# A batched product of attention heads, with its body put under a manual schedule

## The chip, the cores and the metric

The kernel runs on one core of a Trainium2 chip. The metric is the device time of one execution in microseconds (us). The core has five engines with an instruction stream each: PE multiplies matrices, ACT and DVE copy and convert, POOL does too but works on SBUF alone here, and SP issues the transfers between device memory and SBUF. Transfers are carried by 16 DMA engines.

## The reference

Both inputs are float32 with the shape 8 x 12 x 512 x 64 (batch, heads, rows, channels), the output is float32, 8 x 12 x 512 x 512.

```python
def reference(x, y):
    return np.einsum('bhtc,bhsc->bhts', x, y).astype(np.float32)
```

So for each of 96 heads a 512 x 64 matrix is multiplied by the transpose of another one. 25.17 MB are read and 100.66 MB are written.

## The kernel before, in words

The 96 heads form 12 groups of eight (`NG = 12`); inside a group there are two halves `a` of four heads. The work has two kinds of step.

`load(g)` issues two transfers of 1 MB (L63), y and x of group g, into one 2 MB buffer of the pool `dpool`. This pool has six buffers (`NB = 6`), and the results use the same ones.

`prepare(g)` converts the group to bf16 with four casts on POOL (L81) into two buffers of `bpool` (three in all), issues `load(g + 6)` if there is such a group, and then turns the data so that the channels lie on the partitions: eight PE transposes at a time into one `pt` tile of PSUM (L91 for y, L105 for x; two such tiles exist), which DVE (L97, L111) or ACT (L99, L113) copies into `yT` and `xT`. The two halves of y go first, then the two of x; the first half of each goes to DVE and the second to ACT. `prepare` is a Python generator: it stops after each of the four halves, so that its pieces can be woven into something else.

`result(o, steps)` makes one of 48 output blocks (two heads, 2 MB). It has four steps of four matmuls each (L130) into a `pm` tile of PSUM (three exist), and each step's tile is copied to the output buffer by ACT (L137, steps 0 and 2) or DVE (L139, steps 1 and 3). Ahead of each step it takes one piece from `steps`. At the end SP issues the store (L140).

The program text at the bottom runs the two phases:

```python
    for g in range(NB + 1):
        for _ in prepare(g):
            pass
    for o in range(G * NG):
        g = NB + 1 + o
        result(o, prepare(g) if g < NG else iter(()))
```

In the text, then, groups 0 to 6 are prepared first; the pieces of groups 7 to 11 are woven into results 0 to 4, and results 5 to 47 stand alone.

The order in which each engine gets its instructions is not that of the text, however. The tile framework collects the instructions with their dependencies and their wishes for buffers, and a scheduler at compile time lays out each engine's stream; an instruction that is ready in its model can be put ahead of one that stands before it in the text. Semaphore waits are then added for what has to be waited for. In the trace of this kernel twelve matmuls of result 0 (L130) ran at 13.15 to 18.12 us, among the transposes of group 1, and the first evictions (L137, L139) ran at 61.5 us, behind the copies of group 9 (the tenth L113 at 60.60 us, the tenth L111 at 60.37 us). SP's stream held all 24 loads, and then the 48 stores.

Of the kernel before, what the change touches and what calls it, by code (L numbers as in the profile page):

```python
# [1 line left out]

# [5 lines left out]


@with_exitstack  # L10
def kernel(
    ctx: ExitStack,
    tc: tile.TileContext,
    x: bass.AP,
    y: bass.AP,
    out: bass.AP,
):

    nc = tc.nc
    B, H, T, C = x.shape
    _, _, S, _ = y.shape
    P = 128
    G = 4  # L30
    Q = P // G
    R = T // Q
    NG = B * H // (2 * G)
    K = R // 2
    NB = 6
    fp32 = mybir.dt.float32
    bf16 = mybir.dt.bfloat16
    COPY = mybir.ActivationFunctionType.Copy
    assert C * 2 == P and S == T and R == 16 and 4 * R * C == K * S

    xv = x.rearrange("b h t c -> (b h t c)").rearrange("(g a p n) -> g p a n", a=2, p=P, n=R * C)
    yv = y.rearrange("b h t c -> (b h t c)").rearrange("(g a p n) -> g p a n", a=2, p=P, n=R * C)
    ov = out.rearrange("b h t s -> (b h t s)").rearrange("(o p n) -> o p n", p=P, n=K * S)

    const = ctx.enter_context(tc.tile_pool(name="const", bufs=1))
    dpool = ctx.enter_context(tc.tile_pool(name="dpool", bufs=NB))
    bpool = ctx.enter_context(tc.tile_pool(name="bpool", bufs=3))
    xpool = ctx.enter_context(tc.tile_pool(name="xpool", bufs=NG))
    ypool = ctx.enter_context(tc.tile_pool(name="ypool", bufs=NG))
    ptpool = ctx.enter_context(tc.tile_pool(name="ptpsum", bufs=2, space=bass.MemoryType.PSUM))  # L50
    pmpool = ctx.enter_context(tc.tile_pool(name="pmpsum", bufs=3, space=bass.MemoryType.PSUM))

    def buffer():
        data = dpool.tile([P, K * S], fp32)
        return data

    loaded = {}

    def load(g):
        data = buffer()  # L60
        n = 2 * R * C
        for i, v in enumerate((yv, xv)):
            nc.sync.dma_start(data[:, i * n:(i + 1) * n].rearrange("p (a n) -> p a n", a=2), v[g])  # L63
        loaded[g] = [data[:, i * n:(i + 1) * n].rearrange("p (a r c) -> p a r c", a=2, r=R) for i in range(2)]

    for g in range(NB):
        load(g)

    ident = const.tile([P, P], bf16)
    make_identity(nc, ident)  # L70

    made = {}

    def prepare(g):

        halves = []
        for s in loaded.pop(g):
            b = bpool.tile([P, R, 2, C], bf16)
            for half in range(2):
                rows = slice(half * K, (half + 1) * K)  # L80
                nc.gpsimd.tensor_copy(b[:, rows], s[:, :, rows].rearrange("p a r c -> p r a c"))  # L81
            halves.append(b)
        yb, xb = halves
        if g + NB < NG:
            load(g + NB)
        yT = ypool.tile([P, G * Q, R], bf16)
        xT = xpool.tile([P, K, P, 2], bf16)
        for half in range(2):
            pt = ptpool.tile([P, K, P], bf16)
            for k in range(K):  # L90
                nc.tensor.transpose(  # L91
                    pt[:, k, :], yb[:, half * K + k].rearrange("p a c -> p (a c)"), ident
                )
            dst = yT[:, :, half * K:(half + 1) * K]
            src = pt.rearrange("p k n -> p n k")
            if half == 0:
                nc.vector.tensor_copy(dst, src)  # L97
            else:
                nc.scalar.activation(dst, src, COPY)  # L99
            yield  # L100
        for half in range(2):
            pt = ptpool.tile([P, K, P], bf16)
            for k in range(K):
                e, i = divmod(k, K // 2)
                nc.tensor.transpose(  # L105
                    pt[:, k, :], xb[:, e * K + half * K // 2 + i].rearrange("p a c -> p (a c)"), ident
                )
            dst = xT[:, half * K // 2:(half + 1) * K // 2]
            src = pt.rearrange("p (e i) n -> p i n e", e=2)
            if half == 0:  # L110
                nc.vector.tensor_copy(dst, src)  # L111
            else:
                nc.scalar.activation(dst, src, COPY)  # L113
            yield
        made[g] = (xT, yT.rearrange("p n k -> p (n k)"))

    def result(o, steps):

        g, rest = divmod(o, G)
        a, pair = divmod(rest, 2)  # L120
        xT, yT = made[g]
        ot = buffer()
        otv = ot.rearrange("p (r s) -> p r s", s=S)
        for k in range(K // 2):
            next(steps, None)
            pm = pmpool.tile([P, 2, S], fp32)
            for two in range(2):
                for h in range(2):
                    col = (2 * pair + h) * Q
                    nc.tensor.matmul(  # L130
                        pm[h * 64:(h + 1) * 64, two, :],
                        xT[a * C:(a + 1) * C, 2 * k + two, col:col + Q].rearrange("c n e -> c (n e)"),
                        yT[a * C:(a + 1) * C, (2 * pair + h) * S:(2 * pair + h + 1) * S],
                        start=True, stop=True,
                    )
            if k % 2 == 0:
                nc.scalar.activation(otv[:, 2 * k:2 * k + 2, :], pm, COPY)  # L137
            else:
                nc.vector.tensor_copy(otv[:, 2 * k:2 * k + 2, :], pm)  # L139
        nc.sync.dma_start(ov[o], ot)  # L140
        for _ in steps:
            pass

    for g in range(NB + 1):
        for _ in prepare(g):
            pass
    for o in range(G * NG):
        g = NB + 1 + o
        result(o, prepare(g) if g < NG else iter(()))


# [1 line left out]
_INS = ['x', 'y']  # L153
_OUTS = [((8, 12, 512, 512), 'float32')]


# [23 lines left out]
```

## Time and profile before

| what | value |
|---|---|
| median of 4 runs | 308.24 us (307.89 to 308.72) |
| profiled execution, its time | 307.88 us |
| profiled execution, its span | 306.1 us |
| PE busy | 198.7 us (65%) |
| DVE busy | 145.8 us (48%) |
| ACT busy | 119.2 us (39%) |
| POOL busy | 49.3 us (16%), all of it before 68 us |
| moved by the DMA engines | 126.03 MB, 412 GB/s on average |
| a load, from issue to landing | 18.5 to 18.8 us (1 MB) |
| a store, from issue to landing | 26.2 us (2 MB) |

The span is the time from the first to the last instruction in the profiled execution. Busy times overlap, since the engines work side by side; the shares are averages over the whole span. The time from issue to landing of a transfer has its place in the queue in it. The profile's second part cuts the span into 40 slices of 7.65 us.

### The profile page before, as it was taken

Reading aid. Unit: us, or ns where it says so; the run is one execution under the profiler, and the core shown is the slowest. Engines: PE = TensorE matmul, PEld = TensorE weight load, DVE = VectorE, ACT = ScalarE, POOL = GpSimd, SP = SyncE. Lnnn points to the kernel's source line nnn. Section 1 sums busy time; section 2 is a strip of 40 time slices with the busy share of each in tenths; the row PEclk is TensorE's granted clock in tenths of the full one; section 3 lists DMA queues with packets and bytes.
Section 4 is the critical chain, followed back from the end, with each engine's and each line's share of the span. In section 5 each row is a group of like instructions: output and inputs, shape, how many; then the busy total and the mean of one; then the engine's idle time right before and its main releaser. Section 6 shows DMA issues by size and latency. Waiting matters only on the chain.

```text
span 306.1 us, 2985 instructions
## 1 busy us (share of the span) xinstructions
PE 198.7 (65%) x1152; PEld 107.2 (35%) x1152; DVE 145.8 (48%) x120; ACT 119.2 (39%) x121; POOL 49.3 (16%) x54
## 2 busy tenths in 40 slices
PE   1886666699899857767586757676676757671000
PEld 1555555655355423323232323332332323230000
DVE  0434544499777544545454444445454544443000
ACT  1233344399465352433334342525343443422000
POOL 3776777770000000000000000000000000000000
PEclk9999677599555555555555555555555555555555
DMA  7999999979999999999999999999999999999994
GB/s 282 412 411 408 410 408 408 408 321 441 411 430 422 424 430 420 435 415 441 415 437 419 432 426 418 435 424 430 424 424 430 428 413 441 415 439 420 435 422 206
DMA packets 13455, 126.03 MB, mean 412 GB/s; under 512 B 1152, under 2 KB 1152, under 8 KB 7296
## 3 DMA queue, kind: packets, MB, share of 16 engines
q1 hardware_dynamic: 13440, 125.83, 98.3%
q8 instruction: 9, 0.15, 0.2%
q14 instruction: 6, 0.05, 0.0%
HBM read 25.17 MB, written 100.66 MB: 411 GB/s over the span
## 4 chain that ended last, share of the span: by engine, by line
DMA 57%; PE 19%; ACT 7%; DVE 5%; SPq 1%; issue 1%; POOL 1%; ACTq 0%; DVEq 0%; POOLq 0%
DMA out_dram<-data 51%; PE pm L130 11%; DMA data<-in_x_dram 6%; PE pt L105 4%; ACT data L137 4%; PE pt L91 4%; DVE data L139 3%; ACT xT L113 2%; ACT yT L99 1%; DVE yT L97 1%; SPq L63 1%; POOL b L81 1%; ACTq L137 0%; SPq L140 0%; DVEq L139 0%
## 5 line engine op out<-in xcount | busy, mean ns | idle before, releaser
L130 PE MATMUL pm<-yT,xT 64*64 64x512 bf16 x768 | 159.2, 600 | 56.7 <-ACT data L137 52.2
L139 DVE COPY data<-pm 128x1024 f32<-128x1024 f32 x96 | 117.2, 1224 | 96.6 <-DMA out_dram<-data 56.2
L137 ACT ACTIVATE data<-pm 128x1024 f32<-128x1024 f32 x96 | 94.1, 1022 | 119.0 <-DMA out_dram<-data 107.7
L130 PEld LDWEIGHTS <-xT 64*64 64x64 bf16 x768 | 73.0, 148 | 137.7 <-issue 128.6
L81 POOL CAST b<-data 128x1024 bf16<-128x1024 f32 x48 | 48.6, 1040 | 18.1 <-DMA data<-in_y_dram 8.1
L91 PE MATMUL pt<-ident,b 128*128 128x128 bf16 x192 | 18.8, 272 | 16.8 <-POOL b L81 7.9
L105 PE MATMUL pt<-ident,b 128*128 128x128 bf16 x192 | 21.7, 286 | 6.1 <-DVE yT L97 4.9
L111 DVE COPY xT<-pt 128x1024 bf16<-128x1024 bf16 x12 | 14.7, 1223 | 19.6 <-PE pt L105 19.6
L91 PEld LDWEIGHTS <-b 128*128 128x128 bf16 x192 | 16.7, 125 | 20.1 <-issue 11.9
L97 DVE COPY yT<-pt 128x1024 bf16<-128x1024 bf16 x12 | 14.7, 1223 | 17.5 <-PE pt L91 17.5
L105 PEld LDWEIGHTS <-b 128*128 128x128 bf16 x192 | 18.3, 132 | 12.4 <-issue 10.9
L99 ACT ACTIVATE yT<-pt 128x1024 bf16<-128x1024 bf16 x12 | 12.3, 1025 | 22.4 <-PE pt L91 22.4
L113 ACT ACTIVATE xT<-pt 128x1024 bf16<-128x1024 bf16 x12 | 12.3, 1023 | 16.7 <-PE pt L105 16.7
L99 ACT ACT_TABLE_LOAD x1 | 1.3, 1283 | 0.7 <-PEq L164 0.7
masks.py:199 POOL TENSOR_SCALAR_AFFINE_SELECT ident<-ident 128x128 bf16<-128x128 bf16 x1 | 0.3, 292 | 0.1
masks.py:197 POOL MEMSET ident<- 128x128 bf16 x1 | 0.2, 204 | 0.3 <-POOLq L164 0.3
L164 POOL MEMSET const-float32-0.0<- 128x1 f32 x1 | 0.1, 98 | 0.2 <-issue 0.2
L164 POOL MEMSET const-bfloat16-1.0<- 128x1 bf16 x1 | 0.1, 101 | 0.0
L164 POOL MEMSET const-uint8-127<- 128x1 uint8 x1 | 0.1, 101 | 0.0
L164 POOL MEMSET const-float32-1.0<- 128x1 f32 x1 | 0.1, 98 | 0.0
## 6 DMA issues: line engine op xcount, KB each, us to landing
out_dram<-data SPq DMA_DIRECT2D x48, 2048.0 KB, 26.2
data<-in_y_dram SPq DMA_DIRECT2D x12, 1024.0 KB, 18.5
data<-in_x_dram SPq DMA_DIRECT2D x12, 1024.0 KB, 18.8
```

Of the source, the lines that this page charges most:

```text
L63: nc.sync.dma_start(data[:, i * n:(i + 1) * n].rearrange("p (a n) -> p a n", a=2), v[g])
L81: nc.gpsimd.tensor_copy(b[:, rows], s[:, :, rows].rearrange("p a r c -> p r a c"))
L91: nc.tensor.transpose(pt[:, k, :], yb[:, half * K + k].rearrange("p a c -> p (a c)"), ident)
L97: nc.vector.tensor_copy(dst, src)
L99: nc.scalar.activation(dst, src, COPY)
L105: nc.tensor.transpose(pt[:, k, :], xb[:, e * K + half * K // 2 + i].rearrange("p a c -> p (a c)"), ident)
L111: nc.vector.tensor_copy(dst, src)
L113: nc.scalar.activation(dst, src, COPY)
L130: nc.tensor.matmul(pm[h * 64:(h + 1) * 64, two, :], xT[a * C:(a + 1) * C, 2 * k + two, col:col + Q].rearrange("c n e -> c (n e)"), yT[a * ...
L137: nc.scalar.activation(otv[:, 2 * k:2 * k + 2, :], pm, COPY)
L139: nc.vector.tensor_copy(otv[:, 2 * k:2 * k + 2, :], pm)
L164: nc = _bacc.Bacc("TRN2", target_bir_lowering=False, num_devices=1)
```

## The change

The whole body, from the first loads to the last result, is put into `with tc.manual_schedule():`. Inside this block the scheduler does not choose: each engine's stream has the order of the program text. Buffers, dependencies and the instructions themselves are as before. The rest of the diff is indentation; line numbers grow by one.

```diff
-    for g in range(NB):
-        load(g)
+    with tc.manual_schedule():
+        for g in range(NB):
+            load(g)
 
-    ident = const.tile([P, P], bf16)
-    make_identity(nc, ident)
+        ident = const.tile([P, P], bf16)
+        make_identity(nc, ident)
...
-    for g in range(NB + 1):
-        for _ in prepare(g):
-            pass
-    for o in range(G * NG):
-        g = NB + 1 + o
-        result(o, prepare(g) if g < NG else iter(()))
+        for g in range(NB + 1):
+            for _ in prepare(g):
+                pass
+        for o in range(G * NG):
+            g = NB + 1 + o
+            result(o, prepare(g) if g < NG else iter(()))
```

More of the change, by code (lines that the diff above doesn't have):

```diff
@@ L64, in load @@
         loaded[g] = [data[:, i * n:(i + 1) * n].rearrange("p (a r c) -> p a r c", a=2, r=R) for i in range(2)]
-    for g in range(NB):
-        load(g)
-    ident = const.tile([P, P], bf16)
-    make_identity(nc, ident)
[L72 to L78, printed above, removed]
-            for half in range(2):
[L80 to L134, printed above, removed]
-                    )
[L136 to L141, printed above, removed]
-            pass
@@ L144, with prepare, result @@
-    for g in range(NB + 1):
-        for _ in prepare(g):
-            pass
-    for o in range(G * NG):
-        g = NB + 1 + o
-        result(o, prepare(g) if g < NG else iter(()))
+    with tc.manual_schedule():
[3 more added lines that the diff above has]
+        make_identity(nc, ident)
+        made = {}
+        def prepare(g):
+            halves = []
+            for s in loaded.pop(g):
+                b = bpool.tile([P, R, 2, C], bf16)
+                for half in range(2):
+                    rows = slice(half * K, (half + 1) * K)
+                    nc.gpsimd.tensor_copy(b[:, rows], s[:, :, rows].rearrange("p a r c -> p r a c"))
+                halves.append(b)
+            yb, xb = halves
+            if g + NB < NG:
+                load(g + NB)
+            yT = ypool.tile([P, G * Q, R], bf16)
+            xT = xpool.tile([P, K, P, 2], bf16)
+            for half in range(2):
+                pt = ptpool.tile([P, K, P], bf16)
+                for k in range(K):
+                    nc.tensor.transpose(
+                        pt[:, k, :], yb[:, half * K + k].rearrange("p a c -> p (a c)"), ident
+                    )
+                dst = yT[:, :, half * K:(half + 1) * K]
+                src = pt.rearrange("p k n -> p n k")
+                if half == 0:
+                    nc.vector.tensor_copy(dst, src)
+                else:
+                    nc.scalar.activation(dst, src, COPY)
+                yield
+            for half in range(2):
+                pt = ptpool.tile([P, K, P], bf16)
+                for k in range(K):
+                    e, i = divmod(k, K // 2)
+                    nc.tensor.transpose(
+                        pt[:, k, :], xb[:, e * K + half * K // 2 + i].rearrange("p a c -> p (a c)"), ident
+                    )
+                dst = xT[:, half * K // 2:(half + 1) * K // 2]
+                src = pt.rearrange("p (e i) n -> p i n e", e=2)
+                if half == 0:
+                    nc.vector.tensor_copy(dst, src)
+                else:
+                    nc.scalar.activation(dst, src, COPY)
+                yield
+            made[g] = (xT, yT.rearrange("p n k -> p (n k)"))
+        def result(o, steps):
+            g, rest = divmod(o, G)
+            a, pair = divmod(rest, 2)
+            xT, yT = made[g]
+            ot = buffer()
+            otv = ot.rearrange("p (r s) -> p r s", s=S)
+            for k in range(K // 2):
+                next(steps, None)
+                pm = pmpool.tile([P, 2, S], fp32)
+                for two in range(2):
+                    for h in range(2):
+                        col = (2 * pair + h) * Q
+                        nc.tensor.matmul(
+                            pm[h * 64:(h + 1) * 64, two, :],
+                            xT[a * C:(a + 1) * C, 2 * k + two, col:col + Q].rearrange("c n e -> c (n e)"),
+                            yT[a * C:(a + 1) * C, (2 * pair + h) * S:(2 * pair + h + 1) * S],
+                            start=True, stop=True,
+                        )
+                if k % 2 == 0:
+                    nc.scalar.activation(otv[:, 2 * k:2 * k + 2, :], pm, COPY)
+                else:
+                    nc.vector.tensor_copy(otv[:, 2 * k:2 * k + 2, :], pm)
+            nc.sync.dma_start(ov[o], ot)
+            for _ in steps:
+                pass
+        for g in range(NB + 1):
+            for _ in prepare(g):
+                pass
+        for o in range(G * NG):
+            g = NB + 1 + o
+            result(o, prepare(g) if g < NG else iter(()))
```

## The prediction

> **What bounds the kernel now.** I read the page's second part first, because two rows say almost everything.
>
> ```profile
> DMA  7999999979999999999999999999999999999994
> GB/s 282 412 411 408 410 408 408 408 321 441 411 430 422 424 430 420 435 415 441 415 437 419 432 426 418 435 424 430 424 424 430 428 413 441 415 439 420 435 422 206
> ...
> q1 hardware_dynamic: 13440, 125.83, 98.3%
> ```
>
> The transfer engines are full from the second slice to the last but one. Rates are about 409 GB/s while inputs come in, about 427 while results go out. There is one dent inside, the ninth slice (321 GB/s, 61.2 to 68.9 us): here loads end and stores begin. 25.17 MB at 409 plus 100.66 MB at 427 is 61.5 + 235.7 = 297.2 us; the first load is issued at 0.74 us, the last store is followed by a few us of tail, and the span is 306.1. So the dent and the two ends are all that any reordering can win. The windows show the dent close up (columns: PE, PEld, DVE, ACT and POOL busy, clock, DMA share, GB/s).
>
> ```profile
> 62.00:63.00 1.00, 1.00 (x17) 0.79 (x16) 1.00 (x2) 1.00 (x2) 0.91 (x1) 1.00 1.05 418
> 63.00:64.00 1.00, 1.00 (x12) 0.37 (x8) 1.00 (x2) 1.00 (x2) 0.55 (x1) 1.00 0.86 332
> 64.00:65.00 1.00, 0.97 (x13) 0.76 (x12) 1.00 (x2) 1.00 (x2) 1.00 (x2) 1.00 0.16 66
> 65.00:66.00 1.00, 0.96 (x8) 0.46 (x8) 1.00 (x1) 0.59 (x2) 0.53 (x2) 1.00 0.49 209
> 66.00:67.00 1.00, 1.00 (x12) 0.55 (x11) 0.99 (x2) 0.72 (x1) 1.00 (x2) 1.00 0.77 328
> 67.00:72.00 5.00, 4.93 (x46) 2.40 (x43) 4.84 (x5) 4.78 (x5) 0.96 (x1) 1.00 1.00 419
> ```
>
> From 63 to 67 us 0.94 MB moved where 4 x 427 GB/s would have moved 1.71 MB: 0.77 MB, or 1.8 us, is lost. Why, the timeline says (start, us, engine, line, operation; rows of POOL, ACT and SP).
>
> ```profile
> 40.42 2.02 POOL L81 CAST b<-data 128x1024 bf16<-128x1024 f32 x2 [0.54 <-DMA data<-in_x_dram]
> ...
> 60.60 1.02 ACT L113 ACTIVATE xT<-pt 128x1024 bf16<-128x1024 bf16 x1 [1.33 <-PE pt L105]
> 61.52 1.94 ACT L137 ACTIVATE data<-pm 128x1024 f32<-128x1024 f32 x2
> ...
> 65.05 13.22 SPq L140 DMA_DIRECT2D out_dram<-data  x5
> ```
>
> Casts come in pairs, four casts a group, so the pair at 40.42 is the last of group 6, whose buffer is free for result 0 from 42.44. Yet the first eviction of a result (L137) starts at 61.52, with no idle time before it: it was not waiting for a buffer or for the matmuls (twelve of result 0's sixteen ran at 13.15 to 18.1 us), it stood in ACT's order behind the tenth L113 (group 9). The first store is issued at 65.05, when the loads have run out.
>
> **The Trainium skill.** "DMA: Bandwidth & Descriptors", section "Anatomy of one DMA": transfer engines never wait on semaphores, the issuing sequencer does, and a transfer has a fixed cost, mostly completion latency, of about 2 us. The trace agrees in kind: issue of store 0 at 65.05, first of its sixteen completions at 71.16, less the 4.91 between later stores' first completions, leaves 1.2 us. The same page, "Queues, rings and completion order": each ring is consumed in order, so a store issued behind queued loads starts as they end; no gap inside the load phase or the store phase contradicts it. "TensorE: Matmul & The Clock Gate", specification table: ACT, DVE and POOL execute strictly first in, first out; the idle-free L137 above agrees. Its Part 1 says that the array's clock is either half or full; the windows show 0.50 and 1.00, and sixteen transposes take 1.86 or 1.05 us.
>
> **The change, part by part.** Nothing is added or removed: 1152 matmuls and transposes, 240 copies out of PSUM, 48 casts, 72 transfers, the same buffers. Only orders move.
>
> 1. SP. Text order is twelve pairs of loads, then 48 stores. The issue times show exactly this now (L63 0.7 to 47.1, L140 from 65.05). Nothing moves: zero. POOL likewise casts group by group in both.
> 2. PE, early. The twelve matmuls at 13.15 to 18.1 us go behind prepare(6). They held group 1's transposes back, and one POOL wait of 1.94 us at 27.61 follows from the lag. Casts from group 4 on may come 1.4 us sooner. Worth zero: the loads' first completions are 2.56 us apart before and after that wait (1.05 MB at 409 GB/s), so transfers hide it, with seven or so loads queued (18.7 us from issue to landing).
> 3. ACT and DVE. Result 0's evictions now stand behind prepare(6) and half of prepare(7), not behind prepare(9). Group 7's first cast pair starts at 42.98, so its first half is ready at 44.0, and its buffer (group 6's) was free at 42.44. One step of "result with a prepare" costs, per engine: PE 32 transposes and 16 matmuls, at full clock 2 x 1.05 + 2 x 1.05 = 4.2 us, at half clock 2 x 1.86 + 16 x 0.2116 = 7.1 us (100 matmuls took 21.16); DVE 4 x 1.22 = 4.9; ACT 4 x 1.02 = 4.1; data 5.1 a group. I take 5.3 (the dense stretch from 61 to 76 us had the full clock). Result 0 is then evicted at about 49, results 1 to 4 at 55, 60, 65 and 71 us.
> 4. The first store is therefore issued at about 50, and waits in its ring behind some five loads. Loads end at about 63.3 us on the engines' side; store k has to be issued by 62 + 4.91 k: 62, 67, 72, 77, 82. With the times above every one is early, and results 5 onward cost less than 4.91 each (PE 3.4 at half clock). The dent goes.
> 5. From there each result waits for the store six places earlier, as now (ACT at L137 waits 107.7 us in all for stores): no change, the store phase is transfers end to end, and so is the tail.
>
> **Sum.** Dent seen in bytes: 1.8 us. Seen in completions: first completion of the last load at 64.25, of store 0 at 71.16, 6.91 apart instead of 4.91, so 2.0 us for the foremost transfer engine; the last of the sixteen completes 5.64 apart, so 0.73 for the hindmost, which finishes the loads 1.54 us late. That lag is wiped out by the dent now and would be carried into the stores then. Later in the store phase such lags shrink by some 0.07 us a store, and the engine that ends last gained its 3.28 us during the stores, so I count most of it: **1.7 us**. Span 306.1 becomes 304.4; with 1.78 around it (307.88 less 306.1), 306.2 for the profiled execution. The median of the runs shown, 308.24, is 0.36 above that execution: **306.5**, 0.55% less.
>
> **Unpriced.** Evictions running beside casts and loads from 45 to 64 us: the casts at 63.45 and 65.94, beside full DVE and ACT, took 2.02 a pair like all others, so I take zero, with at most 10% on two pairs a group, 0.4 us, hidden under 5.1. A changed start: bounded by the first load's issue at 0.74, so +-0.1.
>
> **Rivals.**
> - *The dent is covered but the hindmost engine decides* (gain 0.73 or less, or the lost time returns as another lag at the end). For: the end is one engine's, 3.28 us behind the first. Against: that lag grew after the dent. Time 307.5 to 308.2.
> - *Starvation, slower.* Text order ties results 0 to 4 to prepare(7) to (11) on PE. At step length p result 4 is ready at 44 + 5p; due at 82, so above p = 7.6 us the rings run empty. At half clock PE alone needs 7.1, and waits for pt and pm buffers, which PE's fixed order exposes, could make it 8.5: ready at 86.5, a hole of 4.5 less the 1.7 won, +2.8: 311.0. For: from 29.5 to 60 us the clock was full in only one window in three, and the load phase's transposes mostly took 1.86. Against: with both kinds of work mixed the clock was full for 17 us.
> - *Nothing happens*: the order stays, or waits for buffers pin the first evictions where they are. The twelve early matmuls contradict the first; the buffer free at 42.44 the second. 308.2.
>
> **Chances.** Dent closed 0.73; hindmost engine 0.10 (half of it within 0.2%); starvation or another slower order 0.13; nothing 0.04. A difference of 0.2% (0.6 us) is about what measurement of this kernel can tell from none. Faster 0.78, same 0.09, slower 0.13. Range: full gain with a spread of the runs, 2.6 below, down to 305.6; upward to the hindmost and the mildest starvation, 308.4.
>
> **What would show it.** Right: L137 first at 44 to 48 us, L140 first issued near 50, no slice under 400 GB/s between the second and the last, no early L130 before L91 of group 6, POOL's wait at 27.6 gone with load spacing still 2.56. Wrong: a dent after 80 us with SP waiting for DVE or ACT (starvation), or a gap closed with an unchanged end (hindmost engine: completions of the last store spread over more than 3.3 us).

## The result: a little faster, because one dent went and another came

The changed kernel takes 307.72 us (median of 38 executions, 307.22 to 307.97), the kernel before 308.22 us beside it (57 executions, 306.91 to 310.08). The ratio over all these executions is 0.9977 with the 95% interval [0.9969, 0.9986]: 0.23% faster (0.16% by the medians), where 0.55% was forecast. Ratios here leave out executions more than 1.5% above the fastest of their kernel; of the kernels here only the one before with doubled transposes (`bwarm`) has such executions. The profiled executions lie closer together, 307.76 against 307.88 us, with spans of 306.0 and 306.1 us.

The second part of the page after, clock (`PEclk`, in tenths of full speed) and transfers:

```profile
PEclk9995555555555555555555555555555555555555
DMA  7999999999889999999999999999999999999995
GB/s 281 412 411 408 410 411 408 409 435 426 379 349 425 427 418 435 413 443 416 435 420 432 422 433 420 424 431 422 433 418 439 418 435 418 433 420 428 433 426 223
```

The ninth slice has gone from 321 to 435 GB/s: the dent between loads and stores is closed. But the eleventh and twelfth slices (76.5 to 91.8 us) have fallen from 411 and 430 to 379 and 349. And the clock row shows the half clock from the fourth slice on, where the kernel before had full stretches until 77 us. Its clock row:

```profile
PEclk9999677599555555555555555555555555555555
```

The windows of the trace after (PE, PEld, DVE, ACT, POOL busy, clock, DMA share, GB/s) show both places:

```profile
63.00:67.00 4.00, 4.00 (x27) 1.96 (x28) 2.36 (x2) 2.07 (x3) 2.03 (x2) 0.50 1.08 450
...
80.00:84.00 4.00, 4.00 (x27) 2.05 (x27) 2.49 (x3) 1.99 (x2) 0.00 (x0) 0.50 0.83 352
84.00:88.00 4.00, 4.00 (x22) 1.82 (x20) 3.04 (x3) 2.13 (x3) 0.00 (x0) 0.50 0.65 274
88.00:92.00 4.00, 4.00 (x22) 2.25 (x20) 2.81 (x3) 2.63 (x3) 0.00 (x0) 0.50 0.93 393
```

From 80 to 92 us PE is busy all the time (12.00 of 12.00 us) and the DMA engines are not: they wait for PE's results. PE's timeline after, one woven step and the head of the next:

```profile
44.45 1.01 PE L92 MATMUL pt<-ident,b 128*128 128x128 bf16 x8 [0.46 <-DVE xT L112]
45.39 1.06 PE L131 MATMUL pm<-yT,xT 64*64 64x512 bf16 x4
46.38 1.04 PE L92 MATMUL pt<-ident,b 128*128 128x128 bf16 x8
47.35 1.06 PE L131 MATMUL pm<-yT,xT 64*64 64x512 bf16 x4
48.34 1.04 PE L106 MATMUL pt<-ident,b 128*128 128x128 bf16 x8
49.31 1.06 PE L131 MATMUL pm<-yT,xT 64*64 64x512 bf16 x4
50.30 1.04 PE L106 MATMUL pt<-ident,b 128*128 128x128 bf16 x8
51.27 1.06 PE L131 MATMUL pm<-yT,xT 64*64 64x512 bf16 x4
52.26 1.04 PE L92 MATMUL pt<-ident,b 128*128 128x128 bf16 x8
```

No row but the first waits for anything. Eight transposes take 0.97 us from start to start (0.94 in the first row), four matmuls 0.99, and the pattern repeats after 7.8 us (44.45 to 52.26). That is PE alone at half clock. SP issues the stores, which are numbered from 0, at the same distance, 7.84 us: 53.66, 61.50, 69.34, 77.18 and 85.02 us.

```profile
53.66 23.86 SPq L141 DMA_DIRECT2D out_dram<-data  x4
...
85.02 13.73 SPq L141 DMA_DIRECT2D out_dram<-data  x5
```

The DMA engines need a store every 4.84 us from about 63 us on.

The dent closed because ACT's first eviction of a result, at 61.52 us before, comes earlier (the matmuls that it needs end at 46.45):

```profile
46.54 1.02 ACT L138 ACTIVATE data<-pm 128x1024 f32<-128x1024 f32 x1 [1.50 <-DMA data<-in_y_dram]
```

In completions (each transfer has sixteen, one for each DMA engine), the first of the last load comes at 64.17, of store 0 at 68.98, so 4.81 us apart instead of 6.91. Then the first completions of stores 3 and 4 are 7.67 us apart, 83.50 to 91.17, where 4.84 would have been full pace: a hole of 2.8 us.

### The profile page after: what moved, and what is told of

The parts are those of the page before. It is cut to its first block, busy times and chain, and to the rows that moved or that the text cites. A ratio compares the mean times of both kernels' runs of the same rounds, so it can differ in the third digit from the quotient of the medians.

```text
span 306.0 us, 2987 instructions
## 1 busy us (share of the span) xinstructions
PE 212.3 (69%) x1152; PEld 110.4 (36%) x1152; DVE 146.1 (48%) x120; ACT 119.8 (39%) x121; POOL 49.4 (16%) x54
## 4 chain that ended last, share of the span: by engine, by line
DMA 58%; PE 24%; DVE 4%; ACT 2%; POOL 2%; issue 1%; SPq 0%; ACTq 0%; POOLq 0%
DMA out_dram<-data 49%; PE pm L131 16%; DMA data<-in_x_dram 9%; PE pt L92 4%; PE pt L106 4%; DVE data L140 3%; ACT data L138 2%; POOL b L82 2%; DVE xT L112 1%; SPq L63 0%; ACTq L138 0%; SPq L141 0%; POOLq L82 0%
## 5 line engine op out<-in xcount | busy, mean ns | idle before, releaser
L131 PE MATMUL pm<-yT,xT 64*64 64x512 bf16 x768 | 167.5, 626 | 48.2 <-ACT data L138 44.6
L138 ACT ACTIVATE data<-pm 128x1024 f32<-128x1024 f32 x96 | 94.8, 1022 | 128.8 <-DMA out_dram<-data 95.2
L92 PE MATMUL pt<-ident,b 128*128 128x128 bf16 x192 | 23.5, 306 | 11.6 <-POOL b L82 8.5
L106 PE MATMUL pt<-ident,b 128*128 128x128 bf16 x192 | 23.9, 302 | 6.0 <-POOL b L82 4.2
L92 PEld LDWEIGHTS <-b 128*128 128x128 bf16 x192 | 19.0, 140 | 20.8 <-POOL b L82 14.6
L106 PEld LDWEIGHTS <-b 128*128 128x128 bf16 x192 | 18.1, 137 | 17.5 <-POOL b L82 10.1
```

Of the source, the lines that this page charges most:

```text
L92: nc.tensor.transpose(pt[:, k, :], yb[:, half * K + k].rearrange("p a c -> p (a c)"), ident)
L106: nc.tensor.transpose(pt[:, k, :], xb[:, e * K + half * K // 2 + i].rearrange("p a c -> p (a c)"), ident)
L131: nc.tensor.matmul(pm[h * 64:(h + 1) * 64, two, :], xT[a * C:(a + 1) * C, 2 * k + two, col:col + Q].rearrange("c n e -> c (n e)"), yT[a * ...
```

## The experiments

Two theories stood after the result. **Starvation**: the woven steps are PE-bound at half clock, and each us by which a store comes late is paid. **Hindmost engine**: only the DMA engine that finishes last counts; the dent was worth 0.7 us to it, the hole cost it 1.3 us, and the rest is lag that comes and goes. Diffs are against the changed kernel unless said otherwise. Each ratio is to executions of the kernel before that were taken beside the run; their medians lie between 308.22 and 308.52 us, so a difference between two changed kernels is uncertain by about 0.3 us.

### One group earlier (w6)

```diff
-            for g in range(NB + 1):
+            for g in range(NB):
...
-                g = NB + 1 + o
+                g = NB + o
```

> Six groups prepared ahead instead of seven; groups 6 to 11 are woven into results 0 to 5. Everything else as in the changed kernel. Starvation theory: the changed kernel's woven results come 7.84 us apart and its fifth store is issued 2.8 us too late (85.24 us, due 82.4 from 64.17 + 5 x 4.84 less the 5.93 from issue to landing). With the weaving one group earlier store 0 is issued at about 48.3 instead of 53.66, store 4 at 79.7, store 5 at 87.5 (due 87.3): the hole at 86 us shrinks from 2.8 to under 0.4 us and the time falls by 2 to 2.8 us, to 304.9 to 305.7. Hindmost theory (the DMA engine that is last decides, and for it the hole cost only 1.3 us): a fall of 0.7 to 1.3 us, to 306.4 to 307.0. If neither hole matters to the end: 307.7.

Measured: 306.00 us (305.97 to 306.24), ratio to the kernel before 0.9913 [0.9891, 0.9936]. Stores were issued at 49.53, 56.41, 64.24, 72.08, 79.92 and 87.76 us, so the step was 7.84 again and the fifth store (store 4) was in time; a hole of 0.6 us was left at store 5. (The changed kernel issued its store 4 at 85.02, not at 85.24.) The fall from the changed kernel is 1.7 us, above what the hindmost theory gave (0.7 to 1.3) and somewhat short of the starvation theory's 2 to 2.8.

### One group later (w8)

```diff
-            for g in range(NB + 1):
+            for g in range(NB + 2):
...
-                g = NB + 1 + o
+                g = NB + 2 + o
```

> Eight groups prepared ahead; groups 8 to 11 are woven into results 0 to 3. Starvation theory: store 0 at about 58.5, store 2 at 74.2 (due 72.8), store 3 at 82.0 (due 77.6): a hole of 4.4 us in all by store 3, against 2.8 in the changed kernel, so 1.6 us slower than it: 309.3. Hindmost theory: a smaller loss, 0.5 to 1 us. If holes do not matter to the end: 307.7.

Measured: 309.98 us, ratio 1.0045 [1.0034, 1.0056]; stores at 58.84, 66.68, 74.53 and 82.37 us. First completions of stores 1 to 2 and 2 to 3 are 6.76 and 7.87 us apart, 4.9 us over full pace in all. The loss against the changed kernel is 2.3 us for 2.1 us more of hole: starvation, not hindmost.

### Two groups earlier (w5), and with a fourth bf16 buffer (w5b4)

```diff
-            for g in range(NB + 1):
+            for g in range(NB - 1):
...
-                g = NB + 1 + o
+                g = NB - 1 + o
```

> Five groups prepared ahead; groups 5 to 11 are woven into results 0 to 6. Starvation theory: store 0 at about 43, the last woven one (store 6) at 90, due 92.1: no hole at all, time 304.9 to 305.5, the same as or 0.3 us below the kernel with six ahead. Hindmost theory: 306.4 to 307.0. If the load phase pays for the earlier matmuls (late casts, late loads): a dent before 64 us and a time over 307.7.

Measured: 312.48 us, ratio 1.0122 [1.0099, 1.0145]. A miss on all counts: the load phase was untouched (slices of 406 to 413 GB/s), but the stores went out at 49.47, 56.87, 65.98, 76.12, 83.96 us and on to store 6 at 99.64. ACT's first evictions of results 1 and 2 waited some 5 us each for casts. I took the three bf16 buffers for the cause and gave it a fourth:

```diff
-    bpool = ctx.enter_context(tc.tile_pool(name="bpool", bufs=3))
+    bpool = ctx.enter_context(tc.tile_pool(name="bpool", bufs=4))
...
-    ypool = ctx.enter_context(tc.tile_pool(name="ypool", bufs=NG))
+    ypool = ctx.enter_context(tc.tile_pool(name="ypool", bufs=NG - 1))
```

> Five groups prepared ahead, as in the kernel that took 312.5 us, but with four bf16 buffers instead of three (ypool gives one of its twelve for the room). In that kernel each woven result waited at its first eviction for its output buffer, which the casts of the next group free, and these waited for a bf16 buffer that only transposes of the same result free: steps of 9 to 10 us. Buffer theory: with a fourth buffer the casts do not wait for this result's transposes, the steps go back to 7.84 us at half clock, store 0 is issued at 45 to 48, store 6 near 93 (due 92.1), a hole of at most 1 us: 305.6 to 306.6. If the bf16 buffers are not the cause: 311 to 313.

Measured: 312.48 us again, ratio 1.0135 [1.0113, 1.0157]. Stores at 49.59, 55.72, 63.56, then 76.18: the steps of results 1 and 2 shrank as the theory said, and result 3 lost it all. ACT's timeline of this kernel there:

```profile
70.85 1.02 ACT L138 ACTIVATE data<-pm 128x1024 f32<-128x1024 f32 x1 [8.55 <-DMA out_dram<-data]
```

Result 3's first eviction waits 8.55 us for a store. The compiled program gives result 3 the buffer of result 0, not the next one that a load leaves (read from its buffer addresses), and store 0 is down at 70.75 us. With three bf16 buffers the same wait stood in the same place (6.09 us, until 70.80). So the buffer theory holds for two steps and not for the time; what decided was that result 3 has its buffer from a store and not from a load.

### The clock (warm), and both remedies together (w6warm)

```diff
-                for k in range(K):
+                for k in list(range(K)) * (2 if g in (5, 6) else 1):
```

(at L91 and L104 of the changed kernel: both loops of transposes)

> The changed kernel with every transpose of groups 5 and 6 done twice (the same values into the same place): 64 extra transposes, 7.5 us of PE at half clock, in the load phase where PE has 1.4 us free per group. They are there to fill whole stretches of PE ahead of the woven results. If that gets the full clock and it lasts through the woven results, the step falls from 7.84 to about 5.1 us (DVE, data), store 4 is issued near 75, the hole at 86 us is gone and the time is 304.9 to 305.7: the half clock was the cause of the long step. If the clock stays at half, store 0 comes 3 to 5 us later, the hole grows to 6 to 8 us and the time is 311 to 313.

Measured: 305.61 us (305.58 to 305.77), ratio 0.9901 [0.9878, 0.9923]. More work, less time. Page and PE's timeline of this kernel:

```profile
PEclk9967599999555555555555555555555555555555
...
GB/s 280 412 411 408 408 410 407 409 431 436 425 427 429 431 431 431 427 431 431 431 429 426 433 429 431 429 436 423 436 425 436 429 427 429 433 427 429 425 438 110
```

```profile
44.87 0.61 PE L92 MATMUL pt<-ident,b 128*128 128x128 bf16 x8 [0.42 <-DVE xT L112]
45.40 0.62 PE L131 MATMUL pm<-yT,xT 64*64 64x512 bf16 x4
```

The clock is full from 37.9 to 75.5 us, eight transposes and four matmuls take about 0.55 us each, the stores go out at 51.01, 56.13, 61.56, 66.35 and 71.39 us, and no slice after the first falls under 400 GB/s until the last. The step is 5.1 us (20.38 us for four), close to the forecast's 5.3, and here its mechanism works undisturbed.

```diff
-            for g in range(NB + 1):
+            for g in range(NB):
...
-                g = NB + 1 + o
+                g = NB + o
...
-                for k in range(K):
+                for k in list(range(K)) * (2 if g in (4, 5) else 1):
```

> The doubled transposes (groups 4 and 5) together with the weaving one group earlier. If there is no hole left to close in the kernel with doubled transposes alone, nothing more is to be had: 305.4 to 305.8, within 0.1% of 305.61. If the lead of the stores itself is worth something: 304.5 to 305.2. If the full clock does not come, the kernel is as the one with the earlier weaving alone or worse: 306.0 to 310.

Measured: 305.65 us (305.51 to 305.86), ratio 0.9919 [0.9901, 0.9937]. No hole left, nothing more to gain; the same as the doubled transposes alone. The step was not short throughout, however. Result 4 has result 0's buffer here, and its first eviction waited 8.83 us for store 0, until 70.73 us. PE stood idle for 7.84 us, the clock was at half from 66.3 us on, and the last two woven stores came at 76.06 and 83.89 us, 7.83 us apart; the lead gathered until then kept them in time.

### Longer runs without more work (runs32)

```diff
-                next(steps, None)
+                for _ in range(4 if k == 0 else 0):
+                    next(steps, None)
```

> The changed kernel with another grain of weaving and no other work: all 32 transposes of a group in front of the first step of its result, then its sixteen matmuls, instead of eight transposes ahead of each four matmuls. If runs of transposes as long as 3.4 us are what brings the full clock (as the doubled ones did), the step falls to 5 to 6 us, the hole is gone and the time is 305.5 to 306.0. If the clock stays at half, PE's work per step is the same 7.2 to 8 us and transposes now also wait for their copies in a row (two pt tiles): 307.5 to 309.5.

Measured: median 309.60 us (305.88 to 309.76), ratio 1.0021 [0.9997, 1.0045]. In the profiled execution the clock stayed at half through the woven part, the steps were 7.9 to 8.4 us and stores 3 and 4 came late. A single execution of twelve took 305.88 us; its mean granted clock was 0.587, where those near 309.6 us with a recorded change had 0.534 to 0.572. That the clock was full in its woven part would fit, but is not shown: it has no profile, and the mean counts all that lies ahead of a trace's first clock record as full (in the profiled execution the first 41.0 us, which alone lift it to 0.57). The five executions with doubled transposes lie within 0.2 us; how long a run has to be was not measured.

### The order on some engines only (mad, mpe), and none at all (bwarm)

```diff
-    with tc.manual_schedule():
+    with tc.manual_schedule(engines={mybir.EngineType.Activation, mybir.EngineType.DVE}):
```

> Manual order for ACT and DVE alone; PE, SP and POOL keep the scheduler's freedom. ACT and DVE get the text's order (first eviction behind seven groups); on PE the scheduler still puts twelve matmuls of results early, among the transposes of group 1, and leaves more transposes in runs of sixteen. Starvation theory: the woven stretch has twelve matmuls less to do, 2.5 us at half clock, so store 4 is issued at about 82.5 instead of 85.0 and the hole shrinks from 2.8 to 0.3 us: 305.8 to 306.3. If the order on ACT and DVE is what costs (evictions in front of copies): as the changed kernel, 307.7 or more.

Measured: 306.02 us (305.87 to 307.27), ratio 0.9935 [0.9912, 0.9957]. The scheduler's PE order has twelve matmuls early and transposes in runs of sixteen; stores at 53.00, 61.26, 66.44, 70.97 and 75.49 us, no dent (4.88 us between the first completions of the last load and of store 0) and no hole. The clock came to full from 62.3 to 76 us, which I had not counted on, so this run does not separate the early matmuls from the clock.

```diff
-    with tc.manual_schedule():
+    with tc.manual_schedule(engines={mybir.EngineType.PE}):
```

> Manual order for PE alone. PE has the text's order, with no early matmuls; ACT and DVE are ordered by the scheduler, whose first evictions stand behind eight groups instead of seven. Starvation theory: PE's woven stretch is the same, 7.84 us a step at half clock, so the hole near 86 us stays within 0.5 us of 2.8 and the time is 307.4 to 308.2. If the order on ACT and DVE was what cost in the changed kernel: 305.6 to 306.3.

Measured: 309.83 us, ratio 1.005 [1.0024, 1.0075], 2.1 us slower than the changed kernel where at most 0.5 was expected. The step was 7.84 us as foretold; what I had not priced is that ACT's first eviction now stands behind group 7's last copy:

```profile
51.37 1.02 ACT L114 ACTIVATE xT<-pt 128x1024 bf16<-128x1024 bf16 x1 [2.90 <-PE pt L106]
52.29 1.94 ACT L138 ACTIVATE data<-pm 128x1024 f32<-128x1024 f32 x2
```

In the changed kernel that eviction ran at 46.54. Store 0 went out at 55.75 instead of 53.66, every following one 2.1 us later, and the time rose by the same 2.1 us. The eviction order matters, then, by the start that it gives to the row of stores.

Against the kernel before, with its own order and only the transposes doubled:

```diff
-            for k in range(K):
+            for k in list(range(K)) * (2 if g in (5, 6) else 1):
```

> The kernel before, without the manual order, with the same doubled transposes of groups 5 and 6. ACT and DVE still have their first evictions behind group 9's copies. If closing the dent at 64 us needs the manual order, the first store is still issued near 65 us or later, the dent stays (6.9 us between the first completions of the last load and of store 0) and the time is 307 to 309, the full clock in the load phase notwithstanding. If the doubled transposes alone are the gain: 305.4 to 306.2.

Measured: ratio 0.9983 [0.996, 1.0005]. Fifteen of twenty executions took 306.32 to 309.34 us, median 307.97, against 308.26 beside them; five took 311.00 to 311.08, and the median of all is 308.73. Doubled transposes alone are not the gain, then: with the manual order they made 305.61. The profiled execution, 311.05, is one of the five: first store at 68.16 us, 10.25 us between the first completions of the last load and of store 0, so the dent is there, and larger. How large it is in the other fifteen no trace shows.

### A hole in the middle (gap)

On top of the doubled transposes:

```diff
-                for two in range(2):
+                for two in list(range(2)) * (36 if (o, k) == (24, 0) else 1):
```

> The kernel with doubled transposes, and result 24's first four matmuls repeated 36 times into the same place: 140 extra matmuls, 29.6 us of PE at half clock, so that the stores run dry once in the middle. Four or five stores stand in the queue, some 20 us, so the hole is 7 to 10 us. Lasting-cost theory: stores follow one another by 4.87 us (mean of the sixteen DMA engines) up to the hole, as in the kernel with doubled transposes, and by 4.91 after it, as in all kernels after their hole, because the hole lets the DMA engines start in step again; the time is 305.6 plus the hole plus up to 0.9 us, less what the hindmost engine's lag gives back (up to 3 us). Rival: the pace belongs to the kernel (its clock, its order, its early lead), and is 4.87 on both sides.

Measured: 313.63 us, 8.0 us over the kernel with doubled transposes; the first completions of stores 23 and 24 are 15.71 us apart, the last ones 12.09. The stores of the mean engine (the mean of a store's sixteen completions) follow by 4.881 us ahead of the hole (stores 7 to 23) and by 4.922 after it (24 to 47); the kernel with doubled transposes has 4.881 in both stretches. The pace does not belong to the kernel. What the hole costs the end is nearer to what the last engine lost (12.09 - 4.9 = 7.2 us) plus 23 x 0.04 than to what the first lost (10.8).

### All together

How late the first completion of store 6 comes in the profiled execution, against 98.10 us in the kernel with doubled transposes, the median time, and the mean engine's distance between stores from store 7 to 47:

| kernel | late, us | time, us | later pace of the stores, mean engine, us |
|---|---|---|---|
| doubled transposes | 0.0 | 305.61 | 4.881 |
| both remedies | 0.0 | 305.65 | 4.881 |
| order on ACT and DVE alone | 0.0 | 306.02 | 4.883 |
| one group earlier | 0.7 | 306.00 | 4.917 |
| the changed kernel | 2.9 | 307.72 | 4.921 |
| long runs | 4.7 | 309.60 | 4.921 |
| order on PE alone | 5.0 | 309.83 | 4.921 |
| one group later | 5.2 | 309.98 | 4.919 |
| two groups earlier | 7.7 | 312.48 | 4.922 |
| the same, four bf16 buffers | 7.8 | 312.48 | 4.921 |

From 0.7 to 7.7 us late, the time rises by 6.48 us: 0.93 us for each us by which the stores come late, whether the start, the order on an engine or a buffer makes them late; from none to 0.7 us late it rises by 0.39. So starvation is the price that the changed kernel pays, and the hindmost theory as I had it is refuted. The rate belongs to holes in this place, where the sixteen engines lie 1.6 to 1.8 us apart: for the hole in the middle, which met engines 3.8 us apart and cost the first of them 10.8 us, the time rose by 8.0. The kernel before lies near the same line with its dent: its store 6 is 2.6 us late in the profiled execution, where the line gives 307.7 us and that execution took 307.88.

## Why the prediction was wrong, point by point

- **What bounds the kernel, and the dent: right.** The transfers fill the span, the dent came from the order on ACT and DVE, and the text order closed it: ACT's first eviction (now L138) moved from 61.52 to 46.54 us, in the stretch foretold, and the load to store distance from 6.91 to 4.81 us. The order on ACT and DVE alone closes it too (4.88 us), and so does the order on PE alone (4.89 us), with which the first eviction comes at 52.29; so what counts is when that eviction comes, and not which order brings it about.
- **Step 1 and the loads in step 2: right.** Load spacing stayed at 2.56 us. But the small reading in step 2 was wrong: POOL's wait at 27.6 us did not go (1.93 us in the profile after, which puts it down to a load), so the twelve early matmuls had not caused it. The fixed cost of about 2 us that the prediction quotes is stated, in the section it names, for transfers that POOL (there: gpsimd) issues; SP issues these, and the traces show 1.2 us, before and after (store 4 with the queue empty: 85.02 to 91.17, less 4.91). The measurement decides; no term of the sum rests on it.
- **Step 3, the length of a woven step, failed.** The term "I take 5.3" measured 7.84 us. I had both ends (4.2 at full clock, 7.1 at half) and took the full clock from one stretch of the kernel before. The half-clock end was itself low: four matmuls in a woven step take 0.99 us from start to start, not the 4 x 0.2116 = 0.85 of the long matmul stream. The doubled transposes show that the clock was the term: with it full, 5.1 us and no hole. The Trainium skill ("TensorE: Matmul & The Clock Gate", Part 1) says that sustained activity releases the throttle; the trace after has PE busy without a break from 44 us on at the half clock, so for this mix busy time alone did not do it. Nor did it for the matmuls by themselves: the 142 that follow the woven steps, from 82.63 us on, took 30.00 us without a break, 0.211 us each, at the half clock.
- **Step 4, "with the above every one is early", failed with it.** Store 4 was issued at 85.02, due at 82. The starvation rival had the mechanism and the place; it got 0.13 with its neighbours and too large a hole (4.5 us at a step of 8.5, against 2.8 at 7.84). Its turning point, 7.6 us, was somewhat high: the start of 44 us in "44 + 5p" was 1.8 us early. 85.02 less 5 x 7.84 gives 45.8, and 51.01 less 5.1 gives 45.9 with doubled transposes; from 45.8 on, the rings run empty above about 7.2 us.
- **The sum was mis-sized as well.** Without the hole the gain is 2.6 to 2.9 us (305.61 against 308.22 and 308.52 beside it), not 1.7. At the mean of the sixteen engines the dent was worth 1.8 us (store 0 completes at 69.46 instead of 71.29 in the changed kernel), and the steady pace of 4.88 instead of 4.92 us another 1.9 over 47 stores; the engine that ends last keeps 2.2 of these 3.7 us, because it lags by 4.1 us behind the mean instead of 2.6. The prediction had no term for a change of pace, and had counted the carried lag only as a loss. Its reading that such lags shrink by 0.07 us a store holds for a few stores only: in the kernel before, the completions of one store lie 2.02 us apart at store 2, 1.68 at store 7 and 3.28 at the last.
- **The measured 0.5 us** is then a won dent less a new hole. In the profiled pair the mean engine ends 0.2 us later and the last one 0.1 us earlier. The rest of the 0.5 us lies in the spread of the kernel before, which goes with the recorded clock: its executions with a mean granted clock of 0.593 or 0.561 (to within 0.001) took 307.7 to 308.5 us, of 0.605 308.4 to 308.7, of 0.574 308.8 to 309.3; 0.586 stands at both ends, at 306.9 to 307.4 and at 309.6 to 309.9. Those of the changed kernel, half-clocked in the woven part in the one that was profiled, keep within 0.8 us. That the timing of the clock's changes makes this spread is inferred from these pairs and was not forced in the kernel before.

## What to carry to other kernels

A stream of stores has a due time for each store, so a reordering that lets the first one start early has to be followed to the last one that shares its engine with other work: at a step of 7.84 us against 4.84, a lead of 9 us was gone before the fourth store after the first. (Store 0 was issued at 53.66 and due at about 62.8 us: its first completion, 68.98, less the 6.15 us that store 4 took from issue to first completion with the queue empty.) Price that step at the slowest clock that the trace shows for such a mix, by rows with the same neighbours, and start the woven part early or bring the clock up before it: one group earlier or 64 redundant transposes made 306.00 and 305.61 us of 307.72. Leaving PE to the scheduler, with the text's order on ACT and DVE alone, made 306.02. And an earlier start is safe only as far as the buffers go that the compiled program assigns.

## What was not expected of the hardware

- Stores follow one another by 4.88 us on the mean engine as long as the queue has never run dry, and by 4.92 after it has, even after one hole of 0.6 us; a hole put into the middle changes the pace at that point. Ahead of a hole the completions of one store lie 1.6 to 3.8 us apart. After it they lie within 0.25 us in most kernels, but 0.8 us apart with long runs and 1.0 with one group earlier, and those two have the longer distance all the same (4.921 and 4.917). That engines in step hinder one another was only argued, and these two speak rather against it; the cause stays open.
- The lag with which the hindmost DMA engine ends the loads does not build up slowly. In all thirteen traces the sixteen completions of a load lie within 0.5 us up to the eighth load and 1.5 to 1.9 us apart from the ninth on (0.24 and 1.67 in the trace after), until the loads end. Just ahead of the ninth, at 24.1 to 24.5 us, the first 16 KB packet of the instruction queue runs, for 1.1 us. That it holds up one engine is inferred from this coincidence.
- Where a trace records no change of the clock, the profile takes it for full. The page with the order on PE alone has no clock row, and its windows say 1.00, while eight transposes take 1.04 us as in the half-clocked trace above:

```profile
56.00:60.00 4.00, 4.00 (x26) 1.91 (x24) 2.38 (x3) 1.94 (x2) 2.02 (x2) 1.00 1.02 409
...
56.31 1.04 PE L92 MATMUL pt<-ident,b 128*128 128x128 bf16 x8
```

The same goes for all that lies ahead of a trace's first record, 29.5 us in the kernel before and 19.4 in the changed one: under the 9 of the first slice sixteen transposes took 2.02 us at 6.76 us of the kernel before. Durations tell which it is.

- The half clock held through nearly 40 us in which PE had no idle time, with eight transposes and four 64-row matmuls in turn; once the clock was full it stayed so through some 25 us of that same mix, with PE idle now and then for up to 0.6 us. Through the idle stretch of 7.84 us in the kernel with both remedies it did not.
